# Recurrent mixer: value and gate of all heads projected ahead of it, by 2x2 blocks with seven products, and kept in DRAM

## The chip, the cores and the metric

The kernel runs on one core of a Trainium2 chip. The metric is the device time of one launch in microseconds (us), the median of several runs. The engines work in parallel, each on a queue of its own that it takes in order, and wait for each other by semaphores: PE (matrix products and transposes), DVE (elementwise), ACT (functions and copies), POOL (elementwise, and some DMA issues) and SP (issues most DMAs). SBUF is the working memory on the chip, PSUM holds the sums of matrix products in eight banks of 128 x 512 float32, DRAM is the large memory outside.

## The reference

The kernel computes two layers of an encoder over 1024 tokens of width 1024, in float32. Layer 0 mixes tokens by window attention, layer 1 by a gated linear recurrence in both directions (HGRN2); each mixer also has four cross-attention heads into 256 memory tokens, and each layer ends with a gated feed-forward block. The change is in layer 1:

```python
def mixer_hgrn2(u, mem_kv, w_in, lb_fwd, lb_bwd, norm_g, w_out):
    ...
    q, i, zf, zb, gate, xq = jnp.split(u @ w_in, [HG_W, 2 * HG_W, 3 * HG_W, 4 * HG_W, 5 * HG_W], axis=-1)
    shp = (bsz, t, HG_HEADS, HG_KEY_DIM)          # 8 heads of 128
    q = jax.nn.silu(q.astype(F32)).reshape(shp)
    v = i.astype(F32).reshape(bsz, t, HG_HEADS, HG_VAL_DIM)
    ...
    lf_f, k_f = forget(zf, lb_fwd)                # log f and 1 - f, f = lb + (1 - lb) sigmoid(z)
    lf_b, k_b = forget(zb, lb_bwd)
    o = (gla_chunked(q, k_f, v, lf_f)
         + flip_t(gla_chunked(flip_t(q), flip_t(k_b), flip_t(v), flip_t(lf_b))))
    o = rmsnorm(o, norm_g.reshape(HG_HEADS, HG_VAL_DIM)).reshape(bsz, t, HG_W).astype(u.dtype)
    o = o * jax.nn.silu(gate)
    return jnp.concatenate([o, memory_cross_attn(xq, mem_kv)], axis=-1) @ w_out
```

So each head needs five projections of `u`: q, the two forget gates f and b, the value v and the output gate.

## The kernel before

**Products.** Each float32 operand is held as a rounded part and a rest (`uh`/`ul` for the normed tokens, `wh`/`wl` for weights), and a product is made by three matmuls (`mm3`, L79 to L83; `mmk`, L568 to L575, in the feed-forward). A weight unit of 128 x 1024 (`wunit`, L69 to L78) is one DMA on SP into one of four stages `st`, a cast on ACT (L76) to `wh`, and a subtraction on DVE (L77) to `wl`; four units are held in a ring. `split` (L85 to L87) is the same for values made on the chip.

**The mixer.** After the first feed-forward, `hgrn()` (L1032) runs head by head. `proj(h)` (L1138) issues the projections of head h in the order of the table `ORD`: an entry such as `f1` is a group of 24 matmuls of 512 columns (8 blocks of the 1024 inputs, three matmuls each) that makes f for the second half of the tokens with features on the partitions (`proj_fm`, L1118), after which ACT and DVE take it from PSUM (`pj`). In every second head the entry `V v01234567` makes value and gate of that head and the next with tokens on the partitions (`proj_tm`, L1096): eight token tiles of 24 matmuls, 192 in all, each evacuated by a DVE copy (L1114), three ACT steps (L1092 to L1094) and a DVE product (L1116) into the SBUF buffers `V` and `G`, which hold three heads.

`head(h)` (L1335) then runs four `direction`s (L1163): forward and backward, for each half of the tokens. A direction is one long chain: ACT (L1178 to L1182), DVE (L1181, L1183, the scan of running sums L1185, L1188), ACT (L1192, L1193, L1205, L1206), DVE products and rescalings (L1207 to L1210, L1220, L1221, L1229), POOL products (L1228, L1246, L1248, L1256), PE score blocks into `pa` (L1213), DVE's masked copy (L1249, L1250), PE transposes (L1259) and state updates `pu` (L1264), and DVE's state recurrence (L1273). Its temporaries `E` are a ring of five. Two `output`s per head (L1276) multiply by the states, norm, gate and transpose. `HX` says after which of the six steps of a head a unit of cross-attention (`cross`, L1324) is put.

**The order.** The program's text is turned into in-order queues by a scheduler that looks at a simulated timeline and at priorities (evacuations of PSUM are put ahead by `AHEAD`). PE is given the projections of head h+1 between the steps of head h. After head 7 the output projection (`wo1`, matmuls into `pb`) goes on; its products stand partly among the last head's steps, as far as free tiles of SBUF allow (`free`, before `wo1.begin`).

**The feed-forward** already uses products of 2 x 2 blocks with seven in place of eight; for them, sums of weight blocks are made in DRAM by POOL DMAs that add to their target (`second_sums`, L128 to L146). For layer 0 these are issued in window attention, each behind a step of the rotary embedding on POOL (L288, L289).

## Time and profile before

| | us |
|---|---|
| median of 3 runs | 2659.72 (2658.41 to 2663.05) |
| the profiled execution's own time | 2659.68 |
| its span, first to last instruction | 2657.9 |
| first projection matmul of the mixer | at 1212.5 |
| first score matmul `pa` of head 0 | at 1255.3 |
| last score matmul `pa` of head 7 | 1893.0 |

The spans of stages are read from the trace by cutting it at such events, and asking for each stretch how long each engine was busy in it. A row of a group of instructions names line, engine, operation, output and inputs, shapes and count, then the busy time, the mean of one in ns, and the idle time of that engine just before them with what ended it. Matmuls are pipelined: a row's mean (0.39 us) is longer than the distance from one to the next.

### The profile page before, as it was taken

What the parts mean: (1) busy time and instruction counts of PE and PEld (TensorE: products, weight loads), DVE (VectorE), ACT (ScalarE), POOL (GpSimd) and SP (SyncE); (2) the same over time, 40 slices, a digit from 0 to 9 for tenths busy, and PEclk for the clock granted to TensorE, in tenths of its full rate; (3) what the DMA queues carried; (4) which work ended last, traced back from release to release, by engine and by line L of the source; (5) the groups of instructions that cost most, each with busy time, mean ns of one, the idle gap of its engine ahead of it and who ended that gap; (6) DMA issues with size and microseconds to landing.
All of it is one profiled execution on the core that took longest, in us unless ns stands there. A gap on an engine that the chain in (4) does not pass through costs nothing. (4 is left out here: it accounts for less than half of the span.)

```text
span 2657.9 us, 39113 instructions
## 1 busy us (share of the span) xinstructions
PE 2602.9 (98%) x14420; PEld 2184.6 (82%) x14420; DVE 1819.4 (68%) x3043; ACT 1377.5 (52%) x2503; POOL 472.3 (18%) x520
## 2 busy tenths in 40 slices
PE   8999999999999999999999999999999999999998
PEld 7888887788888888887888888888887788888887
DVE  6788886578655565478688686887757765656447
ACT  6467676545444445454464554555534444445453
POOL 0321010211111100031224131231311111110013
PEclk9999999999999999999999999999999999999999
DMA  9782232367777856674236351103437778775666
GB/s 353 247 174 56 74 90 81 103 190 195 198 202 193 209 153 222 215 267 146 84 112 154 82 123 52 53 25 108 134 104 196 194 192 210 197 203 170 204 208 236
DMA packets 195729, 425.93 MB, mean 160 GB/s; under 512 B 20049, under 2 KB 56273, under 8 KB 189905
## 3 DMA queue, kind: packets, MB, share of 16 engines
q1 hardware_dynamic: 161552, 324.06, 37.7%
q0 software_dynamic: 24544, 90.19, 16.3%
q10 hardware_dynamic: 9440, 9.19, 1.0%
q8 instruction: 113, 1.85, 0.3%
q14 instruction: 80, 0.65, 0.1%
HBM read 330.04 MB, written 116.39 MB: 168 GB/s over the span
## 5 line engine op out<-in xcount | busy, mean ns | idle before, releaser
L87 DVE TENSOR_TENSOR wl<-st,wh 128x1024 fp32r<-128x1024 f32 (+1 forms) x238 | 262.6, 1109 | 316.6 <-ACT wh L86 288.0
L86 ACT CAST wh<-st 128x1024 fp32r<-128x1024 f32 (+1 forms) x238 | 222.3, 936 | 289.2 <-PE X L575 191.7
L81 PE MATMUL pj<-uh,wh 128*128 128x512 f32 x512 | 202.9, 397 | 4.5 <-DVE q L1130 2.2
L575 PE MATMUL X<-wl,wh 128*128 128x512 f32 x528 | 204.9, 390 | 0.4 <-DVE wl L87 0.4
L575 PE MATMUL X<-wh,wl 128*128 128x512 f32 x528 | 204.9, 389 | 0.0
L82 PE MATMUL pj<-ul,wh 128*128 128x512 f32 x512 | 201.7, 394 | 0.1
L83 PE MATMUL pj<-uh,wl 128*128 128x512 f32 x512 | 201.7, 394 | 0.0
L575 PE MATMUL X<-wh 128*128 128x512 f32 x528 | 198.7, 390 | 0.0
L81 PE MATMUL pj<-wh,uh 128*128 128x384 f32 (+1 forms) x512 | 189.4, 371 | 4.8 <-DVE gs L1116 2.5
L83 PE MATMUL pj<-wh,ul 128*128 128x384 f32 (+1 forms) x512 | 187.0, 366 | 0.0
L82 PE MATMUL pj<-wl,uh 128*128 128x384 f32 (+1 forms) x512 | 186.7, 365 | 0.1
L77 DVE TENSOR_TENSOR wl<-st,wh 128x1024 fp32r<-128x1024 f32 (+1 forms) x91 | 115.6, 1276 | 28.5 <-ACT wh L76 27.8
L575 PE MATMUL V<-uh,wl 128*128 128x512 f32 x336 | 130.7, 389 | 0.0
L575 PE MATMUL V<-uh,wh 128*128 128x512 f32 x336 | 130.7, 389 | 0.0
L575 PE MATMUL V<-ul,wh 128*128 128x512 f32 x336 | 130.7, 389 | 0.0
L76 ACT CAST wh<-st 128x1024 fp32r<-128x1024 f32 (+1 forms) x97 | 97.8, 1014 | 45.5 <-PE pj L82 25.3
L575 PEld LDWEIGHTS X<-wl,wh 128*128 128x128 f32 x528 | 99.1, 188 | 21.2 <-DVE wl L87 0.8
L81 PEld LDWEIGHTS pj<-uh,wh 128*128 128x128 f32 x512 | 96.3, 188 | 24.7 <-DVE q L1130 3.3
L575 PEld LDWEIGHTS X<-wh 128*128 128x128 f32 x528 | 99.1, 188 | 20.7 <-issue 0.2
L575 PEld LDWEIGHTS X<-wh,wl 128*128 128x128 f32 x528 | 99.1, 188 | 20.7
L963 POOL TENSOR_TENSOR c<-c,g 128x512 f32<-128x512 f32 x24 | 43.6, 1836 | 386.2 <-PE X L575 318.0
L83 PEld LDWEIGHTS pj<-uh,wl 128*128 128x128 f32 x512 | 96.3, 188 | 18.7
(413 smaller groups left out, 7225.8 us busy)
## 6 DMA issues: line engine op xcount, KB each, us to landing
st<-hid SPq DMA_DIRECT2D x154, 256.0 KB, 3.0
st<-in_ffw_dram SPq DMA_DIRECT2D x108, 256.0 KB, 3.4
w2s<-in_ffw_dram POOLq DMA_DIRECT2D x24, 1024.0 KB, 8.4
st<-in_ffw_dram SPq DMA_DIRECT2D x46, 512.0 KB, 4.4
hid<-tt SPq DMA_DIRECT2D x88, 256.0 KB, 4.8
st<-w2s SPq DMA_DIRECT2D x88, 256.0 KB, 3.2
sx<-in_ffw_dram SPq DMA_DIRECT2D x84, 256.0 KB, 4.0
sy<-in_ffw_dram SPq DMA_DIRECT2D x42, 512.0 KB, 6.8
```

Of the source, the lines that this page charges most:

```text
L76: act.copy(h[:, :n], raw)
L77: (eng or dve).tensor_tensor(l[:, :n], raw, h[:, :n].bitcast(F32), op=ALU.subtract)
L81: pe.matmul(o, ah, bh, start=first, stop=False)
L82: pe.matmul(o, ah, bl, start=False, stop=False)
L83: return pe.matmul(o, al, bh, start=False, stop=last)
L86: act.copy(h, src)
L87: dve.tensor_tensor(l, src, h.bitcast(F32), op=ALU.subtract)
L575: last = pe.matmul(o, x, y, start=new, stop=e, skip_group_check=not first)
L963: pool.tensor_tensor(y[q][:, t, :], y[q][:, t, :], g3[:, c], op=ALU.mult)
```

## The change

A new phase `values()` stands between the first feed-forward and `hgrn()`. It multiplies the normed tokens with the value and gate weights of all heads, in two passes (s = 0, 1) of 1024 columns, four heads each. In a pass the tokens are cut in two halves and the 1024 inputs in two halves, and the four blocks of the result come from seven products (numbered 1, 2, 5, 6, 7, 3, 4 in the order in which they run) of four token tiles, two weight units and 48 matmuls each. Products 1, 2 and 3 take parts of `uh`/`ul` as they are; 5, 6, 7 and 4 take sums and differences of them (`t5`, `t6`, `t7`, `t4`), which DVE and ACT build once, in pass 0 (`operands`). Their weights are sums of weight blocks, made in DRAM (`vgsum`) by 16 more POOL DMAs in window attention, behind rotary steps that had none (`VG_SUMS`). The results are gated on ACT and DVE and stored to DRAM (`vgd`) by SP's DMAs; all eight PSUM banks are in use.

In `hgrn()`, `proj_tm` is gone. `proj(h)` starts with two DMAs that read v and the gate of head h from `vgd` into `V` and `G`, which now hold two heads. The order of the groups (`ORD`) is the same for heads 1 to 6, the cross-attention units (`HX`) are spread one to a head, cross-attention weights have buffers of their own (`XW`), and the output projection's first free tiles are these and the buffers of `V` and `G`.

In numbers of instructions: PE has 13092 before and 12996 now (96 matmuls fewer), DVE 3045 and 3051, ACT 2181 and 2161, POOL 525 and 541, SP 987 and 1047.

Where the norm ahead of the mixer ends, DVE's queue reads, before (`ul`: split of the normed tokens; `s`: head 0's f from PSUM; `lmx`, `lg`: bounds of the forget gates; last row: first DVE step of the first direction):

```order
L87 TENSOR_TENSOR ul<-pt,uh 128x4x128 x2
L1135 TENSOR_SCALAR s<-pj 128x512
L87 TENSOR_TENSOR ul<-pt,uh 128x4x128 x2
L1071 TENSOR_TENSOR lmx<-lg 128x16
L1057 MEMSET pa 128x512 x2
L1072 TENSOR_TENSOR lg<-lg,lmx 128x32
L1181 SCALAR_TENSOR_TENSOR s<-s,E 128x512
```

and now (`gi`, `tt`: sums on the way to `t5`; `ui`: the result block that gets products 1 and 2):

```order
L90 TENSOR_TENSOR ul<-pt,uh 128x4x128 x3
L1086 TENSOR_TENSOR gi<-uh 128x1024 x2
L1159 TENSOR_TENSOR ui<-pv,ui 128x512
L1087 TENSOR_TENSOR tt<-ul 128x1024 x2
L1159 TENSOR_TENSOR ui<-pv,ui 128x512
L90 TENSOR_TENSOR ul<-pt,uh 128x4x128
L1088 TENSOR_TENSOR gi<-gi,tt 128x1024 x2
L90 TENSOR_TENSOR t5l<-gi,t5h 128x1024 x2
L1077 TENSOR_TENSOR gi<-gi,uh 128x1024 x2
```

The direction's first step has moved behind the whole new phase, and six sums of 1024 columns and two splits take its place. PE's queue at the same place, where product 2 ends and product 5 begins:

```order
L593 MATMUL pv<-wh,uh 128x512
L593 MATMUL pv<-wl,uh 128x512
L593 MATMUL pv<-wh,ul 128x512
L593 MATMUL pv<-wh,t5h 128x512
L593 MATMUL pv<-wl,t5h 128x512
L593 MATMUL pv<-wh,t5l 128x512
```

Nothing stands between them, so that PE's next matmul behind product 2 is the first that reads `t5`.

Inside the loop, DVE's queue in a direction of an early head reads, before:

```order
L1220 TENSOR_TENSOR ER<-ER,EP 128x8x32
L1114 COPY v<-pj 128x2x128
L1221 TENSOR_TENSOR EP<-EP 128x8x32
L1229 TENSOR_TENSOR E<-ER,s 128x4x64
L1220 TENSOR_TENSOR ER<-ER,EP 128x4x64
L1221 TENSOR_TENSOR EP<-EP 128x4x64
L1249 TENSOR_TENSOR ER<-ER,s 128x512
L1116 TENSOR_TENSOR gs<-pj,gs 128x2x128
L1114 COPY v<-pj 128x2x128
L1250 COPY_PREDICATED Az_11380<-gm_11357,pa 128x512
L1181 SCALAR_TENSOR_TENSOR s<-s,E 128x512
```

and now, in the same steps:

```order
L1365 TENSOR_TENSOR ER<-ER,EP 128x8x32
L1366 TENSOR_TENSOR EP<-EP 128x8x32
L1374 TENSOR_TENSOR E<-ER,s 128x4x64
L1280 TENSOR_SCALAR s<-pj 128x512
L1365 TENSOR_TENSOR ER<-ER,EP 128x4x64
L1366 TENSOR_TENSOR EP<-EP 128x4x64
L1394 TENSOR_TENSOR ER<-ER,s 128x512
L1326 SCALAR_TENSOR_TENSOR s<-s,E 128x512
L1395 COPY_PREDICATED Az_12479<-gm_12456,pa 128x512
```

The copies of v and the gate products have left the chain; a group's evacuation (`s<-pj`) stands in their place, and the next direction's first step (L1326, before L1181) comes ahead of the masked copy.

The diff, cut to its core:

```diff
@@ -33,10 +33,14 @@
-HX = [(0, 0, 1, 1, 0, 0), (0,) * 6] * 4
-
-
-ORD = ["QFB q0 f0 b0 q1 f1 b1 V v01234567"] + ["QFB q0 f0 q1 b1 f1 b0", "QFB q0 q1 f0 f1 b1 b0 V v01234567"] * 3 + ["QFB q0 f0 q1 b1|f1|b0"]
+HX = [(0, 0, 1, 1, 0, 0)] + [(0, 0, 1, 0, 0, 0)] * 6 + [(0,) * 6]
+
+
+ORD = ["QFB q0 f0 b0 q1 f1 b1"] + ["QFB q0 f0 q1 b1 f1 b0"] * 6 + ["QFB q0 f0 q1 b1|f1|b0"]
+
+
+VG_SUMS = [(0, ("w", 1, 0)), (1, ("w", 1, 0)), (2, ("w", 0, 0)), (3, ("w", 0, 2)), (0, ("w", 1, 2)), (1, ("w", 0, 0)), (None, None),
+           (2, ("s", 0)), (None, None), (None, None), (3, ("s", 2))]
 
 
...
@@ -123,6 +126,8 @@
             turn()
         return turn
 
+    vgsum = dram.tile([2, 4, 2, P, 1024], F32, name="vgs")
+    vgd = dram.tile([8, 2, P, NT, P], F32, name="vgd")
     w2sum = [dram.tile([NP2, 4, P, 512], F32, name=f"w2s{l}") for l in range(2)]
 
     def second_sums(l):
@@ -142,6 +147,19 @@
                         pool.dma_start(dst, src, accum_op=ALU.add)
                     else:
                         pool.dma_start(dst, src)
+        if l == 0:
+            for i, (k, src) in enumerate(VG_SUMS):
+                ins = yield
+                if k is None:
+                    continue
+                with tc.issue_after(ins.ins):
+                    for x in range(2):
+                        flat = lambda ap: ap.rearrange("u (a b) c -> a u (b c)", a=64)
+                        o, a_ = flat(vgsum[x, k]), flat(vgsum[x, src[1]] if src[0] == "s" else A["wvg"][2 * x + src[1], src[2]:src[2] + 2])
+                        if i < 4:
+                            pool.dma_start(o, a_)
+                        else:
+                            pool.dma_start(o, a_, accum_op=ALU.add)
         while True:
             yield
 
...
+    def values():
+
+
...
+        ti, tj = slice(0, 512), slice(512, 1024)
+        B = {1: (uh[:, :4, ti], ul[:, :4, ti]), 2: (uh[:, 4:, ti], ul[:, 4:, ti]), 3: (uh[:, 4:, tj], ul[:, 4:, tj])}
+        J = (uh[:, :4, tj], ul[:, :4, tj])
+        for k in (5, 6, 7, 4):
+            B[k] = tuple(tp.tile([P, 4, 512], F32R, name=f"t{k}{c}") for c in "hl")
+        half = lambda x, kk: x[:, 2 * kk:2 * kk + 2]
+
...
+        def operands():
+            xs = block("gi")
+            tmp = lambda: op.tile([P, 2, 512], F32, tag="tt", bufs=2, name="tt")
+
+            def more(o, x, part, kk, op_):
+                for c in range(2):
+                    dve.tensor_tensor(o, x, half(part[c], kk).bitcast(F32), op=op_)
+                    x = o
+
...
+            for kk in range(2):
+                x, q = half(xs, kk), tmp()
+                dve.tensor_tensor(x, f32(B[1], 0, kk), f32(J, 0, kk), op=ALU.subtract)
+                dve.tensor_tensor(q, f32(B[1], 1, kk), f32(J, 1, kk), op=ALU.subtract)
+                dve.tensor_tensor(x, x, q, op=ALU.add)
+                out_of(split, 5, kk, x)
+            yield
+            for kk in range(2):
+                x = half(xs, kk)
+                more(x, x, B[3], kk, ALU.add)
+                out_of(nsplit, 6, kk, x)
+            yield
...
+        where = {1: (0, 0), 2: (0, 2), 4: (1, 2)}
+        sums = {5: 0, 7: 1, 6: 2, 3: 3}
+        tags = ("x0", "x1", "x2", "x3", "v0", "v1", "v2", "v3")
+
...
+        def prod(s, k, ps, first):
+            us = {}
+            begins = s == 0 and k == 1
+            for ts in ((0, 1), (2, 3)) if begins else (range(4),):
+                for u in range(2):
+                    if u not in us:
+                        us[u] = wunit(A["wvg"][2 * s + where[k][0], where[k][1] + u] if k in where else vgsum[s, sums[k], u])
+                    wh, wl = us[u]
+                    for t in ts:
+                        m = slice(t * P, (t + 1) * P)
+                        kt = [2 * u, 2 * u + 1]
+                        mmk(ps[t], 2, lambda x: (B[k][0][:, kt[x], m], B[k][1][:, kt[x], m]),
+                            lambda x: (wh[:, x * 512:(x + 1) * 512], wl[:, x * 512:(x + 1) * 512]), first and u == 0)
+
+        def store(s, g, b, y):
+            v = y.rearrange("p t (h x c) -> p t h x c", h=2, x=2)
+            h0 = 4 * s + 2 * g
+            rows = slice(4 * b, 4 * b + 4)
+            for h in range(2):
+                nc.sync.dma_start(vgd[h0 + h, 0, :, rows, :], v[:, :, h, 0, :])
+            tt = op.tile([P, 4, 2, P], F32, tag="tt", bufs=2, name="tt")
+            z = v[:, :, :, 1, :]
+            act.activation(tt, z, AF.Exp, scale=-1.0)
+            act.activation(tt, tt, AF.Ln, bias=1.0)
+            act.activation(tt, tt, AF.Exp, scale=-1.0)
+            dve.tensor_tensor(tt, z, tt, op=ALU.mult)
+            for h in range(2):
+                nc.sync.dma_start(vgd[h0 + h, 1, :, rows, :], tt[:, :, h, :])
+
+        opd = operands()
+        step = lambda: next(opd, None)
+        for s in range(2):
+            X, V = [bank(f"x{t}") for t in range(4)], [bank(f"v{t}") for t in range(4)]
+            prod(s, 1, X, True)
+            ui = block("ui")
+            with tc.high_priority(AHEAD):
+                for t in range(4):
+                    act.copy(ui[:, t], X[t])
+            step()
+            prod(s, 2, V, True)
+            with tc.high_priority(AHEAD):
+                for t in range(4):
+                    dve.tensor_tensor(ui[:, t], V[t], ui[:, t], op=ALU.add)
+            step()
+            V = [bank(f"v{t}") for t in range(4)]
+            prod(s, 5, V, True)
+            gj = block("gj")
+            with tc.high_priority(AHEAD):
+                for t in range(4):
+                    act.activation(gj[:, t], V[t], AF.Copy, scale=-1.0)
+            store(s, 0, 0, ui)
+            step()
+            prod(s, 6, X, False)
+            uj = block("uj")
+            with tc.high_priority(AHEAD):
+                for t in range(4):
+                    act.copy(uj[:, t], X[t])
+            step()
+            prod(s, 7, X, False)
+            with tc.high_priority(AHEAD):
+                for t in range(4):
+                    dve.scalar_tensor_tensor(gj[:, t], X[t], -1.0, gj[:, t], op0=ALU.mult, op1=ALU.add)
+            prod(s, 3, V, False)
+            with tc.high_priority(AHEAD):
+                for t in range(4):
+                    dve.tensor_tensor(uj[:, t], V[t], uj[:, t], op=ALU.add)
+            store(s, 1, 1, gj)
+            prod(s, 4, X, False)
+            gi = block("gi")
+            with tc.high_priority(AHEAD):
+                for t in range(4):
+                    act.activation(gi[:, t], X[t], AF.Copy, scale=-1.0)
+            store(s, 0, 1, uj)
+            store(s, 1, 0, gi)
...
     def hgrn():
         l = 1
...
-        V, G = [late.tile([P, 3, NT, P], F32, name=x) for x in ("v", "gs")]
+        V, G = [late.tile([P, 2, NT, P], F32, name=x) for x in ("v", "gs")]
+        XW = lambda dt: [late.tile([P, 1024], dt, tag=x, bufs=1, name=x) for x in ("xqh", "xql")]
+        XW(F32)
...
-        def proj_tm(h, us, ts):
-
...
         def proj_fm(h, r, us, bws):
             for b, w in bws:
                 ps = psj.tile([P, 512], F32, tag="pj", name="pj")
@@ -1137,12 +1282,14 @@
 
         def proj(h):
 
-            r = {"q": [None, None], "s": [[None, None], [None, None]], "v": V[:, h % 3], "gs": G[:, h % 3]}
+            r = {"q": [None, None], "s": [[None, None], [None, None]], "v": V[:, h % 2], "gs": G[:, h % 2]}
             us = {}
+            for i, x in enumerate((r["v"], r["gs"])):
+                nc.sync.dma_start(x, vgd[h, i])
 
             def load(w):
                 if w not in us:
-                    us[w] = [wunit(A["wvg"][h // 2, u]) for u in range(4)] if w == "v" else wunit(A["wqz"][h, "qfb".index(w)])
+                    us[w] = wunit(A["wqz"][h, "qfb".index(w)])
                 return us[w]
 
             def run(text):
@@ -1357,7 +1502,7 @@
             head(h, cur)
             if h < 7:
                 cur = proj(h + 1)
-        free = [x[:, i].rearrange("p a b -> p (a b)") for i in (2, 0) for x in (V, G)]
+        free = XW(F32) + [x[:, 0].rearrange("p a b -> p (a b)") for x in (V, G)]
         wo1.begin(psj, ("pj",) * 2, {t: free[i // 2][:, (i % 2) * 512:(i % 2 + 1) * 512] for i, t in enumerate(wo1.order)})
         for b in (1, 0):
             wo1.read(range(6, 7), b * 512, (b + 1) * 512, nc.sync)
@@ -1482,6 +1627,7 @@
     wo0.finish()
     x0.release()
     ffn(0, wo0, h2d, True, (0, 1), (0, 1))
+    values()
     late = hgrn()
     wo1.finish()
     late.release()
```

62 lines of the change are left out of this document (36 added, 26 removed).

## The prediction

> **What bounds the kernel now.** I read the page's first part, then the chain, then windows stage by stage, because an average over stages hides where each engine is short.
>
> ```profile
> span 2657.9 us, 39113 instructions
> PE 2602.9 (98%) x14420; PEld 2184.6 (82%) x14420; DVE 1819.4 (68%) x3043; ACT 1377.5 (52%) x2503; POOL 472.3 (18%) x520
> PE 20%; DMA 1%; DVE 1%; POOL 0%; issue 0%; ACT 0%; DVEq 0%; SPq 0%; POOLq 0%; ACTq 0%
> 2103.07 5.44 PE X L575 x24
> ```
>
> PE is busy for 98% of the span. The chain of waits reaches back only through the last feed-forward stage, but there it is PE all the way, and its row of 24 products in 5.44 us gives 0.2267 us for one 512-column matmul. So a matmul less is worth 0.2267 us wherever PE is the engine that ends last. The windows say where that is (us; busy time and count of PE, PEld, DVE, ACT, POOL; granted clock; DMA share; GB/s):
>
> ```profile
> 700.00:900.00 200.00, 200.00 (x884) 165.59 (x883) 115.56 (x124) 91.24 (x117) 27.14 (x31) 1.00 0.79 199
> 1212.50:1255.30 42.80, 41.21 (x195) 32.98 (x195) 36.35 (x66) 22.00 (x41) 9.30 (x14) 1.00 0.32 105
> 1255.30:1894.00 638.70, 629.81 (x5080) 531.99 (x5079) 493.63 (x977) 338.16 (x731) 169.50 (x177) 1.00 0.31 88
> ```
>
> The first row is a feed-forward stage: PE 200.0 of 200, DVE 115.6. The second is the mixer's **front**, from the first projection matmul (1212.5) to the first score matmul (`pa`, 1255.3). The third is its **loop**, from the first to the last `pa`: PE 629.8 of 638.7 (98.6%), DVE 493.6 (77%). PE sets the loop's length, with DVE second. But the loop is not even:
>
> ```profile
> 1369.75:1453.90 84.15, 83.06 (x778) 70.36 (x777) 74.58 (x148) 47.92 (x103) 33.37 (x36) 1.00 0.59 166
> 1453.90:1507.70 53.80, 53.79 (x332) 45.66 (x332) 32.20 (x66) 24.83 (x51) 7.22 (x9) 1.00 0.36 94
> 1531.40:1618.00 86.60, 83.56 (x778) 70.26 (x777) 75.58 (x148) 47.09 (x101) 30.69 (x31) 1.00 0.43 97
> 1694.20:1782.90 88.70, 85.44 (x788) 71.64 (x787) 76.47 (x148) 48.11 (x104) 25.28 (x26) 1.00 0.13 42
> 1550.00:1600.00 50.00, 47.64 (x427) 40.27 (x426) 48.16 (x97) 28.70 (x67) 18.82 (x20) 1.00 0.52 110
> ```
>
> The second of these rows is a stretch with the value-and-gate projection of two heads in it: PE 53.79 of 53.80, DVE 32.2 (60%). The other long ones have none: DVE is busy 0.886, 0.873 and 0.862 of the time, mean 0.874, and PE 0.987, 0.965 and 0.963. In the best 50 us of them (last row) DVE reaches 0.963 and PE gives way to 0.953. The value projection is PE work with little for DVE, and lies now between stretches where DVE is nearly full. The change takes it out of there.
>
> **What the change removes and adds.** Matmuls: 4 x 192 = 768 become 2 x 7 x 48 = 672, so 96 x 0.2267 = 21.8 us of PE go. That would be the whole gain if PE stayed the bound everywhere; the rest asks what it gives back.
>
> *The new front.* 672 x 0.2267 = 152.3 us. Half of the norm's transposes (32) still fall inside it, as now:
>
> ```profile
> 1213.22 1.04 PE L118 MATMUL pt<-ident,nu 128*128 128x128 f32 x8
> 1234.45 0.69 DVE L87 TENSOR_TENSOR ul<-pt,uh 128x512 fp32r<-128x512 f32 x1 [0.17 <-ACT uh L86]
> L609 DVE TENSOR_TENSOR c<-u,c 128x1024 f32<-128x1024 f32 x10 | 12.2, 1219 | 0.0
> 1236.31 0.68 DVE L1181 SCALAR_TENSOR_TENSOR s<-s,E 128x512 f32<-128x512 f32 x1
> 1250.29 0.42 DVE L1229 TENSOR_TENSOR E<-ER,s 128x256 f32<-128x256 f32 x1
> ```
>
> Eight in 1.04 us make 32 of them at most 4.2; I take 3.5. **A wait is added** at the third product. Products 1 and 2 need only `uh`/`ul`: 96 matmuls, 21.8 us, with the transposes 25.3 us from the front's start. Product 5 needs the sum t5. The norm's last split ends now at 1235.1, 22.6 us after the front's start; in the order of DVE, of the six 1024-element sums and differences four stand ahead of that split and two behind, and then the split of t5, of which PE needs the first half. At 1.22 us each (the 1024-element row), with two `ui` additions of 0.7 among them, that is 29 to 30 us if ahead of the split they mostly fill gaps. PE then waits 4 to 5 us; I take 5, with bounds 3 (all in gaps) and 10 (none). Queued behind it on PE is all the rest of the phase. Behind t5 the later sums have a product of 48 (10.9 us) each and are hidden; if DVE fell behind, each would cost its lateness.
>
> From the last product to the first `pa`, 120 projection matmuls (27.2 us) are queued. The first direction's chain starts when the second group is done, 48 matmuls or 10.9 us in, then about 4 us to its first DVE step (copy, two ACT steps); from that step (1236.31) to the last sum that `pa` needs (ends 1250.71) it took 14.4 us. That makes 29.3, a little behind the 27.2. Front: 152.3 + 3.5 + 5 + 29.3 = 190.1 instead of 42.8: **+147.3** us. Weights and stores of the phase are on SP's queue; the feed-forward row above runs PE at 200 of 200 with a DMA share of 0.79, so I cost them nothing. Were one late, all of its wait would show.
>
> *The clock.* PE now waits a few us at a place where it did not. What that does:
>
> ```profile
> 2018.36 0.50 PE L575 MATMUL Y<-uh,wh 128*128 128x512 f32 x1 [2.16 <-ACT wh L76]
> 2020.33 0.63 PE L575 MATMUL Y<-uh,wl 128*128 128x512 f32 x1
> 2020.75 0.63 PE L575 MATMUL Y<-uh,wh 128*128 128x512 f32 x1
> 2019.00:2030.00 11.00, 10.79 (x45) 8.80 (x45) 6.92 (x8) 2.39 (x4) 1.84 (x2) 0.84 0.95 287
> ```
>
> After a wait of 2.16 us matmuls came 0.42 us apart for some us, and the granted clock of 11 us was 0.84: 0.16 x 11, about 1.7 us lost. I add 1.7 for the t5 wait (bounds 0 and 3.4). The Trainium skill, "TensorE: Matmul & The Clock Gate", Part 1: The HAM clock gate, says that the clock halves after an idle window of about 3.4 us and returns after as long a busy one; by that a 5 us wait would cost the same 1.7, and the trace shows the drop already behind 2.16 us.
>
> *The loop.* What DVE loses:
>
> ```profile
> L1114 DVE COPY v<-pj 128x256 f32<-128x256 f32 x32 | 13.3, 417 | 13.7 <-PE pj L83 13.6
> L1116 DVE TENSOR_TENSOR gs<-pj,gs 128x256 f32<-128x256 f32 x32 | 13.3, 416 | 9.0 <-ACT gs L1094 9.0
> L77 DVE TENSOR_TENSOR wl<-st,wh 128x1024 fp32r<-128x1024 f32 x41 | 55.5, 1356 | 9.7 <-ACT wh L76 9.2
> L81 PE MATMUL pj<-wh,uh 128*128 128x512 f32 x251 | 100.2, 399 | 2.5 <-DVE gs L1116 2.5
> ```
>
> Copies 13.3, gate products 13.3, and twelve of the weight splits (heads 2, 4 and 6, four each) x 1.356 = 16.3: 493.6 - 42.9 = 450.7, and I add 2 for first steps of head 0 that now come behind the first `pa`: 453 us of DVE. PE loses 3 x 251 matmuls, 170.7 us, and gets some 17 of the output projection, which come earlier: 638.7 - 170.7 + 3.9 = 472 if it stays as dense as it was. At 472 DVE would be busy 0.96, which only the best 50 us show. So the loop becomes **one in which DVE and PE are nearly equally loaded**, on in-order queues that wait for each other. Its length is 453 over the share that DVE reaches: at 0.874 (the mean of the rows without V) 518; at 0.963 470, so there PE's 472 holds. Neither end is right: in the 0.874 rows PE was still the fuller engine (0.96 to 0.99), so DVE had to wait for it; the 0.963 holds for 50 us only. I take 0.93, a little over the middle because the projections of q, f and b are now spread evenly over the heads: **487 us**, -151.7.
>
> *The tail* gives those matmuls: 17 to 20, -4.6 at most; I take it whole. *The weight sums*: 16 more POOL DMA issues in window attention.
>
> ```profile
> L142 POOL DMA_DIRECT2D w2s<-in_ffw_dram x6 | 5.4, 1045 | 0.0
> L288 POOL TENSOR_TENSOR rq<-t,t 128x320 f32<-128x320 f32 x24 | 22.9, 954 | 243.4 <-DVE t L287 138.4 <-PE ptq L311 26.0 <-PE pt L389 19.1
> ```
>
> At up to 1.05 us each that is 17 us in a stage where POOL idled 243 us ahead of its 24 rope steps, 10 at a time; two issues behind a step end long before the next. I take 0, with bounds 0 and 5 (the two-issue steps nearest to each other).
>
> **Sum** against the profiled execution's 2659.68 us (its span 2657.9; the median of the runs is 2659.72): 147.3 - 151.7 - 4.6 + 1.7 = -7.3, so **2652** us. The loop alone decides: its break-even is 494.3 us, a DVE share of 0.916.
>
> **The rivals.** A measurement of this kernel can tell about 0.2%, 5.3 us, from no change; so faster means a loop under 489 (a share over 0.926), slower one over 499.6 (under 0.907).
>
> *Slower: the DVE queue stays at 0.874.* A direction is a chain of ACT, DVE, POOL and PE steps over five shared buffers; DVE takes its instructions in order, and what it waited for then, it waits for again. The loop is 518, and the sum is 147.3 + 518 - 638.7 - 4.6 + 1.7 = +23.7: 2683. It decides from a share of 0.907 down. For it: three rows that agree within 0.024. Against it: PE was the fuller engine in all three. Chance 0.26.
>
> *The same: DVE's instructions lengthen.*
>
> ```profile
> 1249.44 0.41 DVE L1220 TENSOR_TENSOR ER<-ER,EP 128x256 f32<-128x256 f32 x1
> L1220 DVE TENSOR_TENSOR ER<-ER,EP 128x256 f32<-128x256 f32 x93 | 53.4, 575 | 1.0
> ```
>
> Undisturbed this took 0.41, on average 0.575; the excess over the loop is 93 x 0.165 = 15.3 us, and for the splits 41 x (1.356 - 1.219) = 5.6. If it is time beside POOL's work, then POOL's 169.5 us in 487 instead of 638.7 makes it 1.31 times as much: +6.5 us of DVE, +7 of the loop, and with it the time stays at 2659 to 2660. The Trainium skill, "SBUF — State Buffer", Who interferes with whom, says so: a DVE instruction with two SBUF inputs shares a read port with GpSimd and is blocked while that holds it. Against it: in the rows without V POOL was busy 0.40, 0.35 and 0.28, as dense as 169.5 in 487 (0.35), and what these DVE instructions met was met there. With a share merely at 0.915 it comes to the same end. Chance 0.24 for both.
>
> *Faster: PE stays the bound.* The loop is 472, the t5 wait costs no clock: 147.3 + 472 - 638.7 - 4.6 = -24: 2636, about the 21.8 of the matmuls. For it: 0.963 over 50 us. Against it: DVE would have to hold 0.96 for all 472. Chance 0.15.
>
> That the products do not fall to 672 I leave out: the order has them.
>
> **How the numbers follow.** My forecast 2652 (0.35; its own range 2645 to 2654) and PE as the bound (0.15) make 0.50 for faster; 0.24 for within 0.2%; 0.26 for slower. The range goes from 2636 to the DVE case at 2683; t5 at 10 us (+5) or POOL late (+5) lie inside it.
>
> **What would show it.** Right: a front near 190 us with one PE wait of 3 to 10 us at the third product; a loop near 487 with DVE at 0.93 and PE at about 0.95; a tail some 4 us shorter. Wrong: PE waits at other products or for a weight in the front; a loop with both engines under 0.9, their waits for each other grown; DVE rows of the same shape over 10% longer; more than one drop of the clock; window attention longer by several us.

## The result and the profile after

The changed kernel takes **2725.52 us** (median of 4 runs, 2721.44 to 2728.84) against 2659.92 before: 1.0244 of it, with an interval of 1.0227 to 1.0262. It is slower by 66 us; the forecast was 2652. One execution of the run splitpool further down (2939.6 us, at a granted clock of 0.84) was in the chip's slower state and is left out. Line numbers of the changed kernel are shifted: L1181 is now L1326, L1213 L1358, L1220 L1365, L77 L80.

The page of the changed kernel, its first part and the head of its chain (this execution took 2728.84 us, the longest of the four, so its span differs from that of the kernel before by 69.2 us and not by 66):

```profile
span 2727.1 us, 39066 instructions
PE 2613.6 (96%) x14324; PEld 2186.2 (80%) x14324; DVE 1866.4 (68%) x3049; ACT 1400.7 (51%) x2483; POOL 485.9 (18%) x536
PE 20%; DVE 0%; DMA 0%; POOL 0%; issue 0%; ACT 0%; SPq 0%; DVEq 0%; POOLq 0%; ACTq 0%
```

PE has 96 instructions fewer, is busy 11 us longer, and idle 58 us more. The chain again names only the last feed-forward stage, so it cannot say where that happened. The windows can: first the stage of window attention, before and then after, then the new front in two pieces and the loop (columns as in the prediction; the last `pa` of the kernel before starts at 1893.9, not 1893.0 as in the table of its times):

```profile
0.00:574.10 574.10, 541.92 (x2964) 471.73 (x2965) 421.10 (x1016) 363.26 (x834) 96.58 (x131) 1.00 0.50 151
```

```profile
0.00:589.40 589.40, 548.81 (x2965) 476.87 (x2965) 424.57 (x1016) 362.73 (x834) 110.71 (x147) 0.99 0.59 175
1228.00:1391.90 163.90, 158.28 (x704) 130.21 (x703) 103.13 (x114) 84.78 (x107) 5.29 (x9) 0.99 0.48 146
1391.90:1419.40 27.50, 27.50 (x122) 22.52 (x120) 18.41 (x36) 15.56 (x25) 1.89 (x3) 1.00 0.61 201
1419.40:1964.80 545.40, 493.25 (x4383) 413.49 (x4382) 456.22 (x904) 287.76 (x633) 168.72 (x178) 0.96 0.36 102
```

| stage | before | after | difference | foreseen |
|---|---|---|---|---|
| start to first feed-forward matmul | 574.1 | 589.4 | +15.3 | 0 |
| first feed-forward | 638.4 | 638.6 | +0.2 | 0 |
| front: to the first `pa` | 42.8 | 191.4 | +148.6 | +149.0 with the clock |
| loop: first to last `pa` | 638.6 | 545.4 | -93.2 | -151.7 |
| to the first matmul of the last feed-forward | 115.7 | 113.5 | -2.2 | -4.6 |
| the rest | 648.3 | 648.8 | +0.5 | 0 |
| span | 2657.9 | 2727.1 | +69.2 | -7.3 |

Two rows carry the miss: the loop (58 us too long) and window attention (15 us). In the loop DVE is busy 456.2 us, as worked out (453), but that is 0.836 of it. PE is idle for 52.1 us, where it was for 8.9, and its clock has fallen to 0.96, which at 545 us is some 21 us of matmul time. The waits of PE and of DVE in that loop (in all, times, longest):

```profile
PE pu L1409 <- DVE S L1418: 13.6, 5, 4.9
PE pj L84 <- DVE s L1280: 9.5, 6, 3.8
PE pj L84 <- DVE q L1275: 5.0, 2, 4.8
```

```profile
DVE s L1326 <- ACT E L1324: 27.0, 17, 3.7
DVE s L1280 <- PE pj L86: 11.5, 6, 4.2
DVE wl L80 <- ACT wh L79: 8.8, 6, 6.1
DVE E L1353 <- ACT ER L1338: 8.2, 14, 1.7
DVE Az L1395 <- PE pa L1358: 7.9, 4, 2.7
```

Each of the two waits for the other: PE for DVE's evacuations and states, DVE for projections and scores and for the first step of a direction. No single one is over 6.1 us.

### The profile page after: what moved, and what is told of

Its sections match the earlier page's. It is cut to its first block, busy times and chain, and to the rows that moved or that the text cites. A ratio compares the mean times of both kernels' runs of the same rounds, so it can differ in the third digit from the quotient of the medians.

```text
span 2727.1 us, 39066 instructions
## 1 busy us (share of the span) xinstructions
PE 2613.6 (96%) x14324; PEld 2186.2 (80%) x14324; DVE 1866.4 (68%) x3049; ACT 1400.7 (51%) x2483; POOL 485.9 (18%) x536
## 5 line engine op out<-in xcount | busy, mean ns | idle before, releaser
L89 ACT CAST wh<-st 128x1024 fp32r<-128x1024 f32 (+1 forms) x238 | 222.4, 936 | 294.0 <-PE X L593 195.3
L84 PE MATMUL pj<-uh,wh 128*128 128x512 f32 x448 | 181.3, 405 | 17.6 <-DVE s L1280 9.0
L86 PE MATMUL pj<-uh,wl 128*128 128x512 f32 x448 | 179.5, 401 | 0.0
L85 PE MATMUL pj<-ul,wh 128*128 128x512 f32 x448 | 178.6, 399 | 0.0
L80 DVE TENSOR_TENSOR wl<-st,wh 128x1024 fp32r<-128x1024 f32 (+1 forms) x99 | 121.3, 1229 | 68.2 <-ACT wh L79 66.3
L79 ACT CAST wh<-st 128x1024 fp32r<-128x1024 f32 (+1 forms) x105 | 105.8, 1015 | 92.3 <-PE pv L593 44.1
L84 PEld LDWEIGHTS pj<-uh,wh 128*128 128x128 f32 x448 | 86.0, 192 | 37.8 <-DVE s L1280 10.9
L1373 POOL TENSOR_TENSOR E<-EP,q 128x256 f32<-128x256 f32 x64 | 51.0, 797 | 291.7 <-DVE EP L1366 250.4
L86 PEld LDWEIGHTS pj<-uh,wl 128*128 128x128 f32 x448 | 85.8, 192 | 17.6
L89 ACT CAST wh<-sy 128x1024 fp32r<-128x1024 f32 x42 | 44.1, 1050 | 108.6 <-PE X L593 103.3
L85 PEld LDWEIGHTS pj<-ul,wh 128*128 128x128 f32 x448 | 86.0, 192 | 16.9
```

Of the source, the lines that this page charges most:

```text
L79: act.copy(h[:, :n], raw)
L80: (eng or dve).tensor_tensor(l[:, :n], raw, h[:, :n].bitcast(F32), op=ALU.subtract)
L84: pe.matmul(o, ah, bh, start=first, stop=False)
L85: pe.matmul(o, ah, bl, start=False, stop=False)
L86: return pe.matmul(o, al, bh, start=False, stop=last)
L89: act.copy(h, src)
```

## The experiments

Loop means first to last `pa`; the share is DVE's busy time over it. Kernels whose loops have the same text (after, nolast, moved) gave 545.4, 540.3 and 538.7, so differences of loops under some 7 us say nothing.

| run | time, us | over before (interval) | loop | PE busy | DVE busy | DVE share | clock |
|---|---|---|---|---|---|---|---|
| after | 2725.5 | 1.0244 (1.0227 to 1.0262) | 545.4 | 493.3 | 456.2 | 0.836 | 0.96 |
| nov | 2551.4 | one run | 529.2 | 479.0 | 455.3 | 0.860 | 0.97 |
| tables | 2724.1 | 1.0240 (1.0223 to 1.0257) | 541.8 | 491.9 | 458.0 | 0.845 | 0.96 |
| ring6 | 2735.9 | 1.0274 (1.0258 to 1.0289) | 552.4 | 495.5 | 464.0 | 0.840 | 0.96 |
| nolast | 2713.6 | 1.0196 (1.0180 to 1.0211) | 540.3 | 491.6 | 456.9 | 0.846 | 0.96 |
| moved | 2718.4 | 1.0212 (1.0194 to 1.0229) | 538.7 | 488.8 | 457.3 | 0.849 | 0.97 |
| nosplit | 2713.8 | 1.0203 (1.0186 to 1.0220) | 535.1 | 491.9 | 438.8 | 0.820 | 0.96 |
| fewpe | 2714.0 | 1.0197 (1.0182 to 1.0212) | 530.1 | 440.0 | 461.7 | 0.871 | 0.90 |
| splitpool | 2725.8 | 1.0238 (1.0217 to 1.0258) | 551.8 | 494.7 | 461.8 | 0.837 | 0.95 |
| beforefew | 2611.0 | 0.9814 (0.9799 to 0.9829) | 589.6 | 568.6 | 491.5 | 0.834 | 0.99 |
| r6few | 2704.3 | 1.0167 (1.0151 to 1.0182) | 525.6 | 435.5 | 460.6 | 0.876 | 0.92 |
| half | 2701.4 | 1.0150 (1.0133 to 1.0166) | 597.2 | 567.0 | 478.4 | 0.801 | 0.97 |
| fewboth | 2693.5 | 1.0123 (1.0108 to 1.0138) | 511.3 | 425.9 | 440.0 | 0.861 | 0.94 |
| r6fewboth | 2709.5 | 1.0179 (1.0162 to 1.0196) | 527.0 | 436.3 | 439.1 | 0.833 | 0.91 |
| nocross | 2666.7 | 1.0025 (1.0015 to 1.0034) | 487.5 | 423.1 | 418.3 | 0.858 | 0.93 |

### Is it the loop without the projection, or the new tables?

**nov**: the kernel before, without the projection.

```diff
-            for t in ts[::2]:
-                ps = [psj.tile([P, 2, 2, P], F32, tag="pj", name="pj") for _ in range(2)]
...
+            if h:
+                return
+            dve.memset(V, 0.25)
+            pool.memset(G, 0.25)
...
-                    us[w] = [wunit(A["wvg"][h // 2, u]) for u in range(4)] if w == "v" else wunit(A["wqz"][h, "qfb".index(w)])
+                    us[w] = None if w == "v" else wunit(A["wqz"][h, "qfb".index(w)])
```

> The kernel before, with the value and gate projection left out (its 768 matmuls, their weight loads and evacuations; v and gate are constants set once), everything else as it was, its own tables of order too. Question: is the changed kernel's loop of 545.6 us (first to last pa) a matter of the loop without that filler, or of the tables and buffers that the change brought with it? Theory CHAIN (a direction is a serial chain of steps over five E buffers, and without the projection there is too little other work to wait behind): loop 525 to 560 us, DVE busy 0.80 to 0.87 of it, PE under 0.92. Rival TABLES (the new order of groups, of cross units, the extra buffers cost it): loop 480 to 505 us, DVE 0.90 or more, PE 0.95 or more.

**tables**: the changed kernel with the old tables.

```diff
-HX = [(0, 0, 1, 1, 0, 0)] + [(0, 0, 1, 0, 0, 0)] * 6 + [(0,) * 6]
+HX = [(0, 0, 1, 1, 0, 0), (0,) * 6] * 4
...
-ORD = ["QFB q0 f0 b0 q1 f1 b1"] + ["QFB q0 f0 q1 b1 f1 b0"] * 6 + ["QFB q0 f0 q1 b1|f1|b0"]
+ORD = ["QFB q0 f0 b0 q1 f1 b1"] + ["QFB q0 f0 q1 b1 f1 b0", "QFB q0 q1 f0 f1 b1 b0"] * 3 + ["QFB q0 f0 q1 b1|f1|b0"]
```

> The changed kernel with the tables ORD and HX of the kernel before (without its V entries): two cross units in every second head, the old order of the groups. CHAIN: the loop stays within 10 us of 545.6, the time within 10 us of 2725. TABLES: the loop falls to 480 to 505 us, the time to 2665 to 2685.

The loop of nov, by windows:

```profile
1256.10:1785.30 529.20, 478.95 (x4345) 403.27 (x4344) 455.28 (x901) 285.99 (x631) 163.58 (x175) 0.97 0.33 93
```

Both came out as CHAIN had it, in nov with PE at 0.905 and DVE at 0.860. The length of this loop is to be read beside the 638.6 of the kernel before: there a projection of 768 x 0.2267 = 174 us of PE, with its weights and evacuations, cost the loop only **109.4 us**, for the same loop without it leaves PE idle for 50 us and at a clock of 0.97. This rests on one execution; its whole span (2549.6) is 108.3 shorter, which agrees. Where the 672 matmuls stand now they cost the front 148.6. That is +39.2 of the 69.2 us. The loop's further 16.2 (545.4 against 529.2) are not the tables (541.8). The changed loop runs 38 PE instructions more than nov's (4383 against 4345): matmuls for q, f and b, of which nov makes more ahead of its first `pa`. They are 8.6 us; what the other 7.6 are stays open, near the scatter of 7.

### Window attention

**nolast**: without the last pair of weight sums. **moved**: all sums, the last two pairs at earlier steps.

```diff
-           (2, ("s", 0)), (None, None), (None, None), (3, ("s", 2))]
+           (2, ("s", 0)), (None, None), (None, None), (None, None)]
```

```diff
-VG_SUMS = [(0, ("w", 1, 0)), (1, ("w", 1, 0)), (2, ("w", 0, 0)), (3, ("w", 0, 2)), (0, ("w", 1, 2)), (1, ("w", 0, 0)), (None, None),
-           (2, ("s", 0)), (None, None), (None, None), (3, ("s", 2))]
+VG_SUMS = [(0, ("w", 1, 0)), (1, ("w", 1, 0)), (2, ("w", 0, 0)), (3, ("w", 0, 2)), (0, ("w", 1, 2)), (1, ("w", 0, 0)), (2, ("s", 0)),
+           (None, None), (3, ("s", 2))]
```

> The changed kernel without the last of the weight sums in window attention (the pair of accumulating DMAs behind the rotary step at 381 us; the third product's weights then lack one of their two parts). Theory DMA: that pair fills the DMA queues while SP's load of ul (384 us) waits its turn, ACT waits 7.3 us for it with the key split behind it, and PE loses about 10 us and its full clock; without the pair window attention (start to first feed-forward matmul) takes 574 to 579 instead of 589.4 us, and the time falls by 9 to 15 us. Rival (the lag comes from all sums together or from another order of instructions): window attention stays over 584 us.

> The changed kernel with all weight sums kept, but the last two pairs put at other rotary steps: the first of them where the table had its first gap (about 336 us), the last one at about 358 instead of 381 us, ahead of the step where SP's loads of ul and the key split met it. Theory DMA (the collision at 384 us makes the 15 us): window attention 574 to 580 us instead of 589.4, time 9 to 14 us lower than 2725, as without that pair (2713.6). Rival: the collision moves with the pair (loads of ul stand at 355 and 365 us too) and window attention stays over 584.

The stage in nolast, then in moved; ACT's step that waits for `ul` in the changed kernel, with the 30 us around it; and the same step in nolast:

```profile
0.00:575.70 575.70, 542.15 (x2964) 470.63 (x2965) 423.38 (x1016) 363.45 (x834) 108.09 (x145) 1.00 0.59 176
```

```profile
0.00:585.20 585.20, 548.23 (x2963) 477.73 (x2964) 423.49 (x1016) 363.42 (x834) 109.56 (x147) 0.99 0.59 176
```

```profile
396.79 0.83 ACT L476 CAST uh<-ul 128x768 fp32r<-128x768 f32 x1 [7.28 <-DMA ul<-oT]
384.00:414.00 30.00, 23.65 (x115) 20.57 (x116) 19.49 (x34) 12.70 (x21) 7.73 (x6) 0.83 0.67 165
```

```profile
383.86 0.84 ACT L476 CAST uh<-ul 128x768 fp32r<-128x768 f32 x1 [2.14 <-DMA ul<-oT]
```

Without that pair of 1 MB transfers, which is issued at 381 us, the stage is 575.7. With it, the load of `ul` that SP issues at 384.0 us arrives for ACT's step at 396.8 (in nolast it is issued at 380.3, and the step starts at 383.9), and the key split that PE's transposes need is behind that step in ACT's queue; over those 30 us PE is busy 23.65 and its clock 0.83. Set against nolast, PE is 3.4 us late ahead of this step, 12.7 late behind it and 13.7 at the stage's end, so the step itself took about 9. The nine traces with all sums at these places (after, tables, ring6, nosplit, fewpe, r6few, fewboth, r6fewboth, nocross) have stages of 583.8 to 589.4, so the 15.3 is the upper end of 10 to 15, and the last pair is worth 8 to 14 of it.

Moving the pairs gave 585.2, over the bound of 584 that the rival had. PE now falls behind near 350 and 380 us: ACT waits 4.3 us until 353.0 for a store from `xo` to land, and 4.5 us until 378.1 for a load of `ul`. But 585.2 lies inside the range of the nine, and splitpool, with the same moved sums, has 580.5. So the transfers have a price wherever they were tried, 6 to 11 us when moved, and how much the move saves is not settled. The time of moved (2718.4) is 5 above nolast.

### Which engine holds the loop?

**ring6**: a sixth `E` buffer, the room taken from `on`, which shares `ot`'s.

```diff
-                return early.tile([P, 512], F32, tag="E", bufs=5, name="E")
+                return early.tile([P, 512], F32, tag="E", bufs=6, name="E")
...
-            on = (wo1.w1 if final else wp).tile([P, 4, P], F32, tag="on", bufs=1, name="on")
+            on = (wo1.w1 if final else wp).tile([P, 4, P], F32, tag="on" if final else "ot", bufs=1, name="on")
```

> The changed kernel with six E buffers instead of five (the room comes from on and ot sharing a buffer). CHAIN: a direction's second ACT step no longer waits for the last pa of the direction ahead of it (DVE's wait for it, 27.0 us in the loop, and ACT's wait for pa, 22.7 us, fall by more than half); loop 510 to 532 us, time 2690 to 2712. Rival (the ring doesn't bind, PE's or DVE's queue order does): loop within 7 us of 545.6, the waits only change their names.

The wait of 27.0 us went, as expected, to one of 0.5, and the loop did not shorten. DVE's waits in the loop of ring6:

```profile
DVE s L1280 <- PE pj L86: 24.9, 7, 7.8
DVE wl L80 <- ACT wh L79: 10.3, 6, 7.0
DVE on L1440 <- POOL ors L96: 9.9, 8, 1.6
...
DVE s L1326 <- ACT E L1324: 0.5, 1, 0.5
```

From head 1 on, of the distances from one direction's first `pa` to the next, one in each head is 22 to 42 us (17 to 30 in the changed kernel) and the others 10 to 21, and DVE's wait for projections (`s` from `pj`) has grown from 11.5 to 24.9 us. Five buffers alone do not hold the loop; the wait took another name. What the sharing of `ot`'s buffer costs was not measured by itself.

**nosplit** takes DVE work away, **fewpe** PE work. **splitpool** moves the DVE work to POOL; it starts from moved, with the sums at their earlier steps, and is to be read beside that run's loop of 538.7.

```diff
-                    us[w] = wunit(A["wqz"][h, "qfb".index(w)])
+                    us[w] = whalf(A["wqz"][h, "qfb".index(w)]) if h else wunit(A["wqz"][h, "qfb".index(w)])
...
+        act.copy(h, raw)
+        return h, h
```

```diff
-                    mm3(ps, wh[:, c], wl[:, c], uh[:, k, m], ul[:, k, m], k == 0, k == KT - 1)
+                    (mm2 if h else mm3)(ps, wh[:, c], wl[:, c], uh[:, k, m], ul[:, k, m], k == 0, k == KT - 1)
```

```diff
-                    us[w] = wunit(A["wqz"][h, "qfb".index(w)])
+                    us[w] = wunit(A["wqz"][h, "qfb".index(w)], eng=pool if h else None)
```

> The changed kernel without the DVE splits of the q, f and b weights of heads 1 to 7 (21 splits of 1.28 us, 27 us of DVE in the loop; the rounded part stands in for the rest, PE does all its matmuls). Theory DVE (DVE's queue sets the loop of 545.4 us): loop 515 to 522 us. Theory PE (PE's own work and its waits set it): loop within 8 us of 545. Theory COUPLED (two nearly full in-order queues that wait for each other, neither alone the bound): loop 525 to 536, half of the work taken away.

> The changed kernel with two instead of three matmuls for q, f and b of heads 1 to 7 (rounded weights times rest of the tokens left out: 336 matmuls, 76 us of PE in the loop; DVE and ACT do all their work). Theory PE: loop falls by 70 to 95 us (the work and some of the slow clock), to 450 to 475. Theory DVE: loop within 15 us of 545. Theory COUPLED: falls by 25 to 50 us, to 495 to 520, with DVE at 0.88 to 0.93 and PE idle more than the 52 us of now.

> The kernel of the run moved, with the splits of the q, f and b weights of heads 1 to 7 on POOL instead of DVE (complete computation; 27 us leave DVE's 456, POOL's 169 us grow by 45 to 60). Theory DVE: loop 515 to 525, as with the splits left out. COUPLED: loop 525 to 540. Rival POOL (its steps in a direction's chain, E and qin, come late behind a split of over 2 us): loop 545 or longer, PE's wait for POOL's E over 10 us instead of 3.8.

Their loops, nosplit and then fewpe, and of splitpool PE's wait for POOL and POOL's split, then two DVE rows, each in moved and in splitpool:

```profile
1418.70:1953.80 535.10, 491.90 (x4382) 415.14 (x4382) 438.84 (x883) 288.46 (x633) 165.14 (x176) 0.96 0.36 104
```

```profile
1414.00:1944.10 530.10, 439.97 (x4047) 370.17 (x4046) 461.71 (x905) 286.73 (x633) 171.22 (x178) 0.90 0.37 105
```

```profile
PE pa L1358 <- POOL E L1373: 9.8, 5, 4.1
L80 POOL TENSOR_TENSOR wl<-st,wh 128x1024 fp32r<-128x1024 f32 x19 | 47.0, 2474 | 47.8 <-ACT wh L79 38.1 <-ACT xp L242 5.6 <-ACT kvh L212 4.1
```

```profile
L1366 DVE TENSOR_TENSOR EP<-EP 128x256 f32<-128x256 f32 x93 | 40.6, 437 | 3.7 <-POOL E L1373 0.6 <-DVE ER L1365 0.5
L1366 DVE TENSOR_TENSOR EP<-EP 128x256 f32<-128x256 f32 x93 | 47.4, 510 | 3.1
L1418 DVE SCALAR_TENSOR_TENSOR S<-S,dec,pu 128x128 f32<-128x128 f32 x93 | 31.3, 337 | 2.9 <-PE pu L1409 1.3 <-ACT S L1416 1.3
L1418 DVE SCALAR_TENSOR_TENSOR S<-S,dec,pu 128x128 f32<-128x128 f32 x93 | 31.4, 337 | 2.9 <-ACT S L1416 2.2 <-PE pu L1409 0.3
```

The PE theory falls: 76 us of matmuls less shorten the loop by 15, below what COUPLED gave it and at the edge of theory DVE (within 15), and PE's clock falls to 0.90, which takes part of it back. Of the 27 us that nosplit was to take from DVE, 17 left its busy time and 10 the loop, inside what COUPLED gave, but hardly outside the scatter. In splitpool the loop is 13 us longer than in moved. On POOL a split takes 2.47 us instead of 1.28, and PE's wait for POOL's `E` grows from 3.3 to 9.8. DVE gains nothing either: 19 splits, 24 us, have left it, and yet it is busy 461.8 us instead of 457.3, for other rows of it are longer beside a POOL that is busy 212 us instead of 168 (`EP` from 437 to 510 ns), while the state update, which reads the PSUM tile `pu`, stays at 337.

### The same cuts elsewhere, and both at once

**beforefew** is the cut of fewpe in the kernel before, **r6few** fewpe with six buffers, **half** the phase for heads 0 to 3 alone.

```diff
-        for s in range(2):
+        for s in range(1):
...
-ORD = ["QFB q0 f0 b0 q1 f1 b1"] + ["QFB q0 f0 q1 b1 f1 b0"] * 6 + ["QFB q0 f0 q1 b1|f1|b0"]
+ORD = ["QFB q0 f0 b0 q1 f1 b1"] + ["QFB q0 f0 q1 b1 f1 b0", "QFB q0 q1 f0 f1 b1 b0"] + ["QFB q0 f0 q1 b1 f1 b0", "QFB q0 q1 f0 f1 b1 b0 V v01234567"] * 2 + ["QFB q0 f0 q1 b1|f1|b0"]
...
-            for i, x in enumerate((r["v"], r["gs"])):
+            for i, x in enumerate((r["v"], r["gs"]) if h < 4 else ()):
```

> The kernel before with two instead of three matmuls for q, f and b of heads 1 to 7 (rounded weights times rest of the tokens left out: 336 matmuls, 76 us of PE in the loop), the same cut that took 15 us from the loop of the changed kernel (545.4 to 530.1). If PE sets the loop of before, as its 98.6% says, the loop of 638.6 falls by 55 to 76 us, to 563 to 584, and the time to 2584 to 2605. Rival (there too a direction's chain is what lasts, and PE is merely kept busy by filler): loop falls by less than 35.

> The changed kernel with six E buffers and with that cut of 336 matmuls, both at once. Alone, the sixth buffer made three directions of a head come 12.5 us apart but the fourth wait 25 to 40 us (loop 552), and the cut alone gave 530. Theory TWO LIMITS (five buffers hold a direction to about 16.5 us; with six, PE's queue, which brings the last projection late, holds the head to 66 us; each hides the other): loop 455 to 490 us, DVE over 0.94. Rival ONE CHAIN (something else holds a head at 64 to 66 us, its single-buffered states or its outputs): loop 515 to 535.

> A mixed form, complete: the phase only for heads 0 to 3 (one pass, 336 matmuls, 8 sums in window attention), value and gate of heads 4 to 7 in the loop as before, with the tables and buffers of the kernel before. Front 112 to 116 us (76.2 + 3.5 + 5.5 + 27.3) instead of 42.8 before. Theory FILLER (without the projection the loop keeps a head at 66 us whatever PE has to do, with it PE is filled): heads 0 to 3 about 66 each, heads 4 to 7 about 82 each as before, loop 585 to 600, time 2675 to 2695. Rival PE (the loop is PE's work and a constant share of waits): loop 472 + 87 over 0.90, about 620, time 2700 or more.

beforefew lies between its two theories: the loop falls by 49.0 (638.6 to 589.6), the time by 49.6, of 76. The same 336 matmuls are worth 49 us where the projection stands beside them and 15 where it does not: PE set the loop before, though not with a wide margin, and does not set it now. r6few (525.6) agrees with its rival: the buffers and PE together do not free it either. half has the loop that FILLER gave (597.2), but heads 0 to 3 (69 to 80 us each) and 4 to 6 (72 to 93) do not separate as cleanly as it said, and the time (2701.4) missed its 2675 to 2695 and is what the rival gave, since window attention took 583.1 with the half of the sums. Half of the change costs about 40 us.

**fewboth** joins nosplit and fewpe, **r6fewboth** adds the sixth buffer, **nocross** leaves the cross-attention out.

```diff
-HX = [(0, 0, 1, 1, 0, 0)] + [(0, 0, 1, 0, 0, 0)] * 6 + [(0,) * 6]
+HX = [(0,) * 6] * 8
...
+        for h, b in units:
+            nc.sync.dma_start(oT[1][8 + h, :, b * 512:(b + 1) * 512], uh[:, h, b * 512:(b + 1) * 512].bitcast(F32))
```

> The changed kernel with both cuts of heads 1 to 7 at once: without the 21 DVE splits of q, f and b (27 us of DVE) and with two instead of three matmuls for them (76 us of PE). Alone they gave loops of 535.1 and 530.1 instead of 545.4. Theory DVE SHARE (in-order waits hold DVE to about 0.87 as soon as PE is out of the way, so the loop is DVE's work over 0.87): DVE 440 us, loop 500 to 512. Theory ADDITIVE (two small effects side by side): 517 to 523. Rival LATENCY (the length of a direction's chain holds it, not the work on DVE): 524 to 532.

> The same with six E buffers (without the DVE cut this stood at 525.6). DVE SHARE: 490 to 508, little below the run with five. LATENCY: if the next direction's first steps run ahead and the chain was what held it, 470 to 490.

> The changed kernel without the eight units of cross-attention in the loop (their output rows are filled with copies of the normed tokens): about 74 us of PE go, about as much as in the cut of two instead of three matmuls, but with them some 50 us of DVE and their ACT steps, work that stands between the steps of a direction. DVE SHARE: DVE 406 us, loop 460 to 480. LATENCY: loop 510 to 530, as with the PE cut alone.

Their loops, fewboth and then nocross:

```profile
1417.90:1929.20 511.30, 425.85 (x4047) 358.04 (x4046) 440.04 (x885) 287.14 (x633) 162.87 (x177) 0.94 0.38 108
```

```profile
1414.10:1901.60 487.50, 423.09 (x3989) 356.01 (x3988) 418.28 (x801) 253.44 (x531) 163.62 (x176) 0.93 0.37 106
```

fewboth came to 511.3, inside DVE SHARE and near its upper end. Taking from both engines gives 34 us where the two alone gave 10 and 15, which is 8 or 9 more than their sum and little over the scatter of 7. In nocross about as much PE work goes as in fewpe, and 38 us of DVE and 34 of ACT with it: the loop falls by 58 instead of 15. It stayed above the 460 to 480 of DVE SHARE, but LATENCY with its 510 to 530 is out. With five buffers, then, DVE's work counts once PE has less to do: beside fewpe's loop, 22 us of DVE less are 19 of the loop in fewboth. What ACT's 34 us do in nocross was not tried alone. With six buffers the same cut of DVE gains nothing (525.6 in r6few, 527.0 in r6fewboth, at a share of 0.833), which fits neither theory; there, as in ring6, one direction of a head comes late (18 to 41 us behind the one ahead of it). Over all variants DVE never came over 0.876 of a loop. Which of DVE's many short waits keep it there was not taken apart further, and that cause stays open.

## Why the prediction was wrong

**The cost of the phase was right.** The front was put at 190.1 us and 1.7 for the clock, and took 191.4: the phase 163.9 where 162.5 was foreseen with the clock, and 27.5 from its last product to the first `pa` instead of 29.3. Its wait was sized right and placed wrong, so the agreement in size is in part luck. PE and DVE there:

```profile
1255.77 0.49 PE L593 MATMUL pv<-wh,uh 128*128 128x512 f32 x1 [4.78 <-DVE ul L90]
1256.91 0.63 PE L593 MATMUL pv<-wh,uh 128*128 128x512 f32 x1
1257.34 0.63 PE L593 MATMUL pv<-wl,uh 128*128 128x512 f32 x1
...
1259.73 0.39 PE L593 MATMUL pv<-wl,uh 128*128 128x512 f32 x1
1259.96 0.39 PE L593 MATMUL pv<-wh,ul 128*128 128x512 f32 x1
...
1261.58 0.40 PE L593 MATMUL pv<-wh,t5h 128*128 128x512 f32 x1
1252.00:1264.00 12.00, 8.23 (x29) 6.65 (x30) 12.00 (x13) 3.38 (x4) 0.00 (x0) 0.86 0.01 1
```

```profile
1249.21 2.35 DVE L1086 TENSOR_TENSOR gi<-uh 128x1024 f32<-128x1024 f32 x2
1252.08 2.35 DVE L1087 TENSOR_TENSOR tt<-ul 128x1024 f32<-128x1024 f32 x2
1254.94 0.68 DVE L90 TENSOR_TENSOR ul<-pt,uh 128x512 fp32r<-128x512 f32 x1
1257.88 2.36 DVE L90 TENSOR_TENSOR t5l<-gi,t5h 128x1024 fp32r<-128x1024 f32 x2
```

The four sums that the order puts ahead of the norm's last split did not fill gaps: they held that split back to 27.6 us after the front's start (22.6 before), and the last 18 matmuls of product 2 waited 4.78 us for it. When PE came to `t5` at 1261.58 it was there. The clock over these 12 us was 0.86, which is the 1.7 us that was put in. The Trainium skill, "TensorE: Matmul & The Clock Gate", Part 1: The HAM clock gate, gives some 3.4 us of busy time until the full clock returns; here the matmuls stood 0.43 apart behind the wait (1256.91 and 1257.34) and 0.23 from 1259.73 on, 4.0 us after its end at 1255.77.

**The loop's length is the step that failed**: "I take 0.93, a little over the middle", and with it 487 us. DVE's work was right (456.2 against 453), the share was 0.836, below the 0.874 that was the low end. Both ends came from a misreading of where the value projection stands. Its matmuls are those of the row `pj<-wh,uh` and of its two fellows (256 each in the whole kernel). Their count, first in the stretch 1369.75:1453.90, which the prediction reads as one of those that "have none", then in 1453.90:1507.70, which it reads as the one with the projection in it:

```profile
L81 PE MATMUL pj<-wh,uh 128*128 128x512 f32 x48 | 19.0, 397 | 0.7 <-DVE gs L1116 0.7
L81 PE MATMUL pj<-wh,uh 128*128 128x512 f32 x16 | 6.4, 403 | 0.0
L81 PE MATMUL pj<-uh,wh 128*128 128x512 f32 x47 | 18.6, 396 | 0.0
```

Each of the three rows "without V" holds 3 x 48 = 144 matmuls of the projection, 32.6 us; the row "with V" holds 48, and 140 of q, f and b (`pj<-uh,wh` and its two fellows). The four stretches that run from the first to the last matmul of a pair of heads' projection (1251.54 to 1305.05, of which the first 4 us lie ahead of the loop, 1410.29 to 1466.48, 1574.50 to 1630.80, 1738.50 to 1795.45), summed, and then the four stretches between and behind them:

```profile
sum 222.95, PE 217.37 PEld 180.97 DVE 180.81 ACT 117.53 POOL 78.86; mean PE 54.34 PEld 45.24 DVE 45.20 ACT 29.38 POOL 19.72
sum 419.41, PE 416.10 PEld 353.77 DVE 316.29 ACT 222.29 POOL 93.05; mean PE 104.03 PEld 88.44 DVE 79.07 ACT 55.57 POOL 23.26
```

With the projection DVE is busy 0.81 and PE 0.975, without it DVE 0.75 and PE 0.99: the opposite of "PE work with little for DVE" between stretches where DVE is nearly full. The projection filled PE beside directions that already kept DVE at 0.87, and the change took PE work away there; the stretches that PE alone fills had none of it to give. So no row showed what DVE would reach once the projection is gone, and nothing carried the step from 0.874 up to 0.93; when PE's work was cut as well, DVE's share was 0.83 to 0.876. That this is how the 174 us came to cost 109 is argued from these rows; the 109 itself is shown by nov.

**No price for PE's clock in the loop.** The sum had 1.7 us for one wait. Its 472 "if it stays as dense as it was" were 463 us of matmuls and the old loop's 8.9 of idle. PE is now idle 43 us more than that, over many waits of 1 to 5 us. Its busy time is 493.3, 30 more than the 463: 5.4 of these are 24 matmuls that the sum left out (the front now holds 120 of head 0's 144 for q, f and b, and the others came into the loop), and 25 are slower matmuls, of which the loss of 0.04 of the clock over 545 us accounts for some 21. 472, 43, 5 and 25 make the 545.

**The weight sums** were put at 0, bounds 0 and 5, from POOL's idle time. POOL had the room; the price lay with the transfers, which met a load of SP's, and was 15.3 in this trace and 10 to 15 over the nine. The step failed in looking at the queue that issues and not at what the transfers run beside.

**The tail** gave 2.2 of its 4.6.

**The rivals.** The slower one had the right sign, and its share of 0.874 is near the most that DVE reached in any variant, though the three rows behind it are the misread ones; with the loop at 518 and no cost in window attention it ended at 2683. In the changed kernel the one with longer DVE instructions is out:

```profile
L1365 DVE TENSOR_TENSOR ER<-ER,EP 128x256 f32<-128x256 f32 x93 | 53.4, 574 | 1.5
L80 DVE TENSOR_TENSOR wl<-st,wh 128x1024 fp32r<-128x1024 f32 x26 | 33.3, 1284 | 10.5 <-ACT wh L79 8.8 <-PE pt L1444 1.7
```

574 ns where it was 575, and 1284 where it was 1356, with POOL busy 0.31 of the loop instead of 0.27. The rule of the Trainium skill, "SBUF — State Buffer", Who interferes with whom, added nothing to the time here. DVE's instructions were longer beside a busier POOL in splitpool alone. PE as the bound (2636) would have needed a loop that no run of the complete kernel came near.

No complete version that was run beats the kernel before.

## What to carry to other kernels

A block of matmuls on a full PE is worth less than its PE time when other engines catch up beside it: leave it out of the old kernel first and see what the loop gives back (109 us of 174 here), and only that can be spent elsewhere. Before a stretch is read as one with a block or without it, count that block's own matmuls in it: here the two were taken for each other. When two engines in a loop are both nearly full and wait for each other in order, do not expect the second one to fill up when the first has less to do: over these variants DVE's share stayed between 0.80 and 0.876. Large transfers that are issued in a stage by an engine with time to spare still need a look at which loads stand behind them.

## What was not expected of the hardware

PE's mean clock over the whole loop fell when PE had less to do, in the changed kernel with no single wait of PE over 5 us: 1.00 at 98.6% busy in the loop before, 0.96 after, 0.90 where PE had 76 us less to do (fewpe). The busy share alone does not set it: fewboth has 0.94 at about the same share (0.83) as fewpe. In fewpe PE's 440.0 us of busy time in 530.1 us are only 53.3 less than in the changed kernel, though the matmuls taken out were worth 76 at the full clock: a part of what is taken from PE comes back as slower matmuls.
